# Means of squares by full-width products with ones, and the root by logarithm, exponential and a Newton step

## The chip, the cores and the metric

One core of one Trainium2 chip runs the whole kernel. The metric is the device time of one execution in microseconds. The kernel before takes 2461.68 us, the median of three runs (2461.52 to 2463.72). Single-precision data throughout; the large products are made as three products of high and low parts of the operands, so that their sum has single precision.

## The reference

One layer of a hybrid decoder, for a prompt of 1024 tokens and 8 single-token samples that share the weights: a combined input projection, three branches (a gated short convolution, a Mamba-2 state-space scan with 32 heads in 4 groups, and cross-attention to 256 memory tokens), gates, a merging projection, and a SwiGLU feed-forward network. The change touches two norms of it:

```python
def rmsnorm(x, w, eps=RMS_EPS):
    y = xf * lax.rsqrt(jnp.mean(xf * xf, axis=-1, keepdims=True) + eps)
    return (y * w)

y_ssd = (y_ssd + ssm_d[:, None] * xs) * jax.nn.silu(z)
y_b = group_rmsnorm(y_ssd, ssm_norm_w, SSM_GROUPS) @ w_ssm_out   # 4 groups of 512 channels
...
xp = xp + h
xp = xp + swiglu(rmsnorm(xp, norm_ffn_w[l]), w_ffn_gate[l], w_ffn_up[l], w_ffn_down[l])
```

## The kernel before

**Layout.** Channels lie on the 128 partitions, tokens along the free axis: 1024 of the prompt and 8 of the samples, 1032 columns (`TT`), in three pieces of 344 (`CW`) for the large products of TensorE (`gemm`, L205) or, in the feed-forward part, two halves of 516 (`HT`), each of 2 x 258 (`HC`). A norm over channels is therefore a sum over partitions.

**Order.** The program is emitted as a list of background pieces (`pend`) that are woven between the products of `gemm`: at certain k-steps of a product the next piece is emitted (`tick`). A `None` in the list lets one such place pass. A scheduler then sets each engine's order by its own plan of times. Each engine runs its queue strictly in order; an instruction that waits holds up all behind it. DMAs that the code issues on `SY` go through SyncE's queue (SP), also in order.

**The state-space stage.** For each head group `g` (512 channels, four tiles `xg[0..3]` of 128x1032) `load_group` (L1376 to L1380) loads the x tiles from `xs_d`, `ssd_pieces` runs eight chunks of 128 tokens (each begins with four transposes of x, `xp`, L989), and at the group's end `z_pieces` adds the skip term (L1112, on DVE), multiplies by the gate (L1115, DVE), squares on ACT (L1120, L1122) and sums the four squares into one tile `sqa` (L1123, DVE). `group_norm` follows:

- `sums` (L1136 to L1144): nine products with a block of 128 columns of `sqa` as the stationary operand and a single column of ones as the moving one (`psny`), which leave the sums with tokens on partitions, 128x9; then on these few values the mean, Sqrt on ACT (with a load of its table), reciprocal and a Newton step on DVE.
- `spread` (L1152 to L1156): nine transposes of the roots, each broadcast along the free axis, which turn them back to tokens along the free axis on all partitions (`psnr`); ACT copies them into `sqa`.
- `scale` (L1160, L1163): four DVE operations x = x * weight * root, and a store of each tile to `yb_d` on SP. The x tiles of the next group use the buffers of these tiles, and their loads (L1380) stand behind the stores on SP.

The other engines' work in this time: TensorE runs the products of the projections `wq` (`ps_q`) in group 0 and of the output projections `wo` (`po`) in groups 1 to 3, DVE the low parts of their weights (L155) and activations (L165), ACT the high parts, exponentials of the scan (L969), and evictions. After the last group come the transposes of the q rows of the samples (`psqr`, copied by ACT into `qrows`) and of the keys (`pskT`, evicted by ACT into `kTh`), the loads of the first keys and values (`kv_ahead`) and cross-attention. Small PSUM tiles (`sm_ps`: psny, psnr, xp, psqr, pskT and others) have two buffers.

**The feed-forward norm.** The merging products (L1823) write the sum x tile by tile; `norm_half` (L1766 to L1786) does the same as above for one half of the columns: six products (`psf`, L1772), the root on 128x6 values, six transposes (`psr`, L1785), two ACT copies into `rf`. Half 0 is woven into the merging products of half 1; half 1 comes just ahead of the first products of the feed-forward network (`g0e`, `u0e`, L253). `normed` (L1790) then scales x, and its forms (high and low parts, sums of blocks for Strassen products) feed those products.

**Engines.** The names in the profile: PE is TensorE, DVE is VectorE, ACT is ScalarE, POOL is GpSimd, SP is SyncE. In the state-space stage GpSimd has small scalings of 128x512 (L1000, L1049).

Of the kernel before, what the change touches and what calls it, by code (L numbers as in the profile page):

```python
# [12 lines left out]
ALU = mybir.AluOpType  # L13
# [30 lines left out]
def tile_kernel(ctx: ExitStack, tc, a, o):  # L44
# [53 lines left out]
    def rsqrt(pool, out, src, n, shape, name):  # L98
# [7 lines left out]
        V.scalar_tensor_tensor(out, t, 1.5, out, op0=ALU.add, op1=ALU.mult)  # L106

# [317 lines left out]
    with tc.tile_pool(name="p0", bufs=1) as p0:  # L425
# [27 lines left out]
        for key, src, n in (  # L453
            ("mem", a["norm_mem_w"], 8),
            ("ffn", a["norm_ffn_w"], 8),
            ("scw", a["sc_conv_w"], 24),
            ("scb", a["ssm_conv_b"], 24),
            ("ssn", a["ssm_norm_w"], 16),
# [650 lines left out]
    def z_pieces(g, xg, hold):  # L1109
        def piece(t):  # L1110
            zs = hold.pop(t)
            V.scalar_tensor_tensor(  # L1112
# [6 lines left out]
            if t == 0:  # L1119
                S.activation(sqa[:, :TT], xg[t], AF.Square)  # L1120
            else:
                S.activation(zs, xg[t], AF.Square)  # L1122
                V.tensor_add(sqa[:, :TT], sqa[:, :TT], zs)  # L1123
# [5 lines left out]
    def group_norm(g, xg, hold):  # L1129

        starts = [i * P for i in range(NCK)] + [TT - P]

        def sums():
            ps = sm_ps(f"psny{g}")
            for i, c in enumerate(starts):
                PE.matmul(ps[:, i : i + 1], hold["q"][:, c : c + P], ones[:, 0:1], start=True, stop=True)  # L1136
            t = hold["r"] = ev_tile(f"nr{g}")
            r, v, s_ = t[:, :9], t[:, 9:18], t[:, 18:27]
            V.tensor_scalar(v, ps[:, :9], 1.0 / 512, EPS, op0=ALU.mult, op1=ALU.add)
            S.activation(s_, v, AF.Sqrt)  # L1140
            V.reciprocal(r, s_)
            V.tensor_mul(s_, r, r)
            V.scalar_tensor_tensor(s_, v, -0.5, s_, op0=ALU.mult, op1=ALU.mult)
            V.scalar_tensor_tensor(r, s_, 1.5, r, op0=ALU.add, op1=ALU.mult)  # L1144

        def spread():
            n = hold["n"] = hold["q"]
            for half in range(2):
                ps = sm_ps(f"psnr{g}{half}")
                for i in range(4):  # L1150
                    j = half * 4 + i
                    PE.transpose(ps[:, i * P : (i + 1) * P], bc(hold["r"][:, j : j + 1], [P, P]), ident)  # L1152
                S.copy(n[:, half * 512 : (half + 1) * 512], ps)
            ps = sm_ps(f"psnr{g}2")
            PE.transpose(ps[:, :P], bc(hold["r"][:, 8:9], [P, P]), ident)
            S.copy(n[:, T:TT], ps[:, P - NS : P])  # L1156

        def scale():
            for t in range(4):
                V.scalar_tensor_tensor(  # L1160
                    xg[t], xg[t], par("ssn", g * 4 + t), hold["n"][:, :TT], op0=ALU.mult, op1=ALU.mult
                )
                SY.dma_start(yb_d[g * 4 + t], xg[t])  # L1163

        return [sums, None, spread, scale]
# [312 lines left out]
    for g in range(GROUPS):  # L1478
# [8 lines left out]
        if g == GROUPS - 1:  # L1487
            norm[1] = lambda: kv_ahead(0)
# [277 lines left out]
    def norm_half(half, sq):  # L1766
        rfs[half] = ev_tile(f"rf{half}")
        t = rfs[half]
        starts = [n * HC + c for n in range(2) for c in (0, P, HC - P)]
        ps = sm_ps(f"psf{half}")  # L1770
        for i, c in enumerate(starts):
            PE.matmul(ps[:, i : i + 1], sq[:, c : c + P], ones[:, 0:1], start=True, stop=True)  # L1772
        r, v = t[:, 600:606], t[:, 606:612]
        s_ = t[:, 612:618]
        V.tensor_scalar(v, ps[:, :6], 1.0 / D, EPS, op0=ALU.mult, op1=ALU.add)
        S.activation(s_, v, AF.Sqrt)
        V.reciprocal(r, s_)
        V.tensor_mul(s_, r, r)
        V.scalar_tensor_tensor(s_, v, -0.5, s_, op0=ALU.mult, op1=ALU.mult)
        V.scalar_tensor_tensor(r, s_, 1.5, r, op0=ALU.add, op1=ALU.mult)  # L1780
# [423 lines left out]
```

## Time and profile before

| | |
|---|---|
| median of three runs | 2461.68 us |
| profiled execution, its own time | 2464.7 us |
| its span | 2463.0 us |
| granted TensorE clock, mean | 0.999 of full |
| ScalarE busy | 1084.4 us (44%) |
| group norms: last add of group 0, 1, 2, 3 starts at | 1076.61, 1167.24, 1250.33, 1339.80 us |
| feed-forward norm, first product of half 0 and 1 | 1715.21 and 1762.17 us |
| TensorE's largest wait in the state-space stage and attention | 2.6 us, for the first attention products (`psa`) |

Times are from one profiled execution, counted from the start of its span. A row of the timeline gives the start, the duration, the engine, the source line, the operation, what it writes and reads, and how many of its kind were merged into the row; brackets give the idle time of the engine just before it and what ended that. One single-precision product is two MATMUL instructions in such a row.

### The profile page before, as it was taken

How to read it: one execution, taken by the hardware profiler on the slowest of the kernel's cores; microseconds unless marked ns; L12 is line 12 of the kernel's file. 1: busy time of each engine (PE TensorE's matmuls, PEld its weight loads, DVE VectorE, ACT ScalarE, POOL GpSimd, SP SyncE). 2: the span in 40 equal slices, each digit the busy share in tenths (PEclk: the TensorE clock that was granted, in tenths of full speed). 3: DMA queues.
4: the chain of work that ended last, by engine and by line, in shares of the span. 5: the costliest groups of instructions: out<-in, count | busy, mean ns of one | idle time of the engine just before them, and what ended most of it. 6: DMA issues, size and time to landing. Idle time of an engine off the chain costs nothing.

```text
span 2463.0 us, 45791 instructions
## 1 busy us (share of the span) xinstructions
PE 2426.6 (99%) x19020; PEld 2363.1 (96%) x19020; DVE 1599.3 (65%) x2589; ACT 1084.4 (44%) x1747; POOL 107.4 (4%) x163
## 2 busy tenths in 40 slices
PE   8999999999999999999999999999999999999998
PEld 6999999999999999888998988999999999999998
DVE  6744677777777675568677763554777555567855
ACT  6634555455453543656555442213443333343423
POOL 0000000000000000212211000000000000000000
PEclk9999999999999999999999999999999999999999
DMA  6355323444343345767886897855444323254621
GB/s 206 129 164 161 121 86 110 133 138 129 115 152 116 108 123 178 219 219 256 266 279 214 267 316 239 275 192 162 145 153 131 102 92 106 89 184 145 189 88 76
DMA packets 359606, 404.81 MB, mean 164 GB/s; under 512 B 16110, under 2 KB 286046, under 8 KB 359391
## 3 DMA queue, kind: packets, MB, share of 16 engines
q1 hardware_dynamic: 334374, 339.69, 44.2%
q10 hardware_dynamic: 25025, 62.21, 6.7%
q8 instruction: 149, 2.44, 0.4%
q14 instruction: 58, 0.48, 0.1%
HBM read 286.74 MB, written 115.32 MB: 163 GB/s over the span
## 4 chain that ended last, share of the span: by engine, by line
PE 85%; DMA 6%; DVE 5%; ACT 3%; issue 1%; SPq 0%; DVEq 0%; ACTq 0%; POOL 0%
PE po L205 11%; PE pm L1823 4%; PE ps_q L205 3%; PE pss L1036 1%; PE py L1023 1%; DMA qb<-qs_d 1%; PE ps_z L205 1%; PE po L1015 1%; DMA in<-yb_d 1%; PE G16m L253 1%; PE Z14m L253 1%; PE Z2m L253 1%; PE d00m L253 1%; PE d16m L253 1%; PE d14m L253 1%
## 5 line engine op out<-in xcount | busy, mean ns | idle before, releaser
L968 ACT ACTIVATE r<-r,acum 128x128 f32<-128x128 f32 x256 | 79.1, 392 | 4.2 <-DMA r<-ac_d 3.5
L758 DVE SCALAR_TENSOR_TENSOR ax<-u,prm,ax 128x1024 f32<-128x1024 f32 x44 | 56.4, 1281 | 0.4 <-ACT ax L755 0.3
L909 ACT ACTIVATE st<-st,es 128x128 f32<-128x128 f32 x128 | 41.3, 392 | 26.1 <-DMA st<-in_state_ssm_dram 21.5
L1000 POOL TENSOR_TENSOR xdd<-xdt,decst 128x512 f32<-128x512 f32 x32 | 37.1, 1159 | 290.6 <-DVE xdt L996 290.6
L994 DVE TENSOR_TENSOR r<-r,cbm 128x1024 f32<-128x1024 f32 x32 | 39.1, 1223 | 2.2
L911 DVE SCALAR_TENSOR_TENSOR st<-sr,dts,st 128x128 f32<-128x128 f32 x128 | 40.2, 347 | 0.4
L1019 DVE TENSOR_TENSOR y<-po,ea 128x512 f32<-128x512 f32 x28 | 19.3, 688 | 28.4 <-PE po L1015 27.1
L915 DVE SCALAR_TENSOR_TENSOR sr<-st,sr 128x128 f32<-128x128 f32 x128 | 35.4, 287 | 1.1
L1456 DVE TENSOR_TENSOR yr<-po,yr 128x1032 f32<-128x1032 f32 x8 | 9.8, 1230 | 40.3 <-PE po L205 22.6
L1023 PE MATMUL py<-r,xdt 128*64 128x128 f32 x512 | 35.0, 279 | 0.0
L1036 PE MATMUL pss<-xdd,bT 128*128 128x512 f32 x64 | 34.2, 616 | 0.7 <-ACT bT L993 0.4
L1830 DVE TENSOR_TENSOR x<-pm,xT 128x516 f32<-128x516 f32 x16 | 11.1, 695 | 36.2 <-PE pm L1823 36.2
L969 ACT ACTIVATE r<-r 128x1024 f32<-128x1024 f32 x32 | 33.9, 1058 | 0.7
L1049 POOL TENSOR_TENSOR s<-s,cdec 128x512 f32<-128x512 f32 x28 | 33.1, 1182 | 2.4 <-DVE s L1042 2.2
L993 ACT COPY bT<-bp 128x128 f32<-128x128 f32 x32 | 8.5, 264 | 54.3 <-DVE cbm L991 54.2
L1023 PEld LDWEIGHTS py<-r,xdt 128*64 128x64 f32 x512 | 27.3, 136 | 4.2 <-issue 0.9
L1752 DVE TENSOR_TENSOR gt<-po,gt 128x1032 f32<-128x1032 f32 x8 | 9.9, 1233 | 32.1 <-PE po L205 30.6
L1557 DVE SCALAR_TENSOR_TENSOR kc<-kc,qb 128x256 f32<-128x256 f32 x64 | 23.7, 421 | 9.7 <-DMA qb<-qs_d 8.3
L1015 PE MATMUL po<-bc,s 128*128 128x128 f32 x224 | 29.8, 276 | 0.0
L1015 PEld LDWEIGHTS po<-bc,s 128*128 128x128 f32 x224 | 28.3, 191 | 0.6 <-DVE s L1042 0.5
L755 ACT ACTIVATE ax<-u,prm 128x1024 f32<-128x1024 f32 x22 | 27.4, 1246 | 2.3 <-DVE u L368 1.1
L761 DVE SCALAR_TENSOR_TENSOR ax<-u,prm,ax 128x1032 f32<-128x1032 f32 x22 | 28.3, 1289 | 0.0
(9217 smaller groups left out, 9097.9 us busy)
## 6 DMA issues: line engine op xcount, KB each, us to landing
r<-ac_d SPq DMA_DIRECT2D x32, 512.0 KB
gt_d<-G ACTq DMA_DIRECT2D x24, 516.0 KB
gt<-gt_d SPq DMA_DIRECT2D x24, 516.0 KB
xs_d<-ax ACTq DMA_DIRECT2D x22, 516.0 KB
x<-xs_d SPq DMA_DIRECT2D x16, 516.0 KB
zs<-zs_d SPq DMA_DIRECT2D x16, 516.0 KB
yb_d<-x SPq DMA_DIRECT2D x16, 516.0 KB
in<-yb_d SPq DMA_DIRECT2D x16, 516.0 KB
```

Of the source, the lines that this page charges most:

```text
L205: PE.matmul(ps[:, n, :CW], wt[:, ks], x[:, n * CW : (n + 1) * CW], start=(k == 0 and i == 0), stop=(k == nk - 1 and i == 2),)
L253: PE.matmul(ps[:, n, :HC], wt[:, ks], x[:, n * HC : (n + 1) * HC], start=(start and kt == 0 and i == 0), stop=(kt == 3 and i == 2), skip_g ...
L758: V.scalar_tensor_tensor(acc[:, :T], u[:, j : j + T], w[j], acc[:, :T], op0=ALU.mult, op1=ALU.add)
L909: S.activation(st[:, i], st[:, i], AF.Copy, scale=es[:, g * 4 + i, b : b + 1])
L911: V.scalar_tensor_tensor(st[:, i], rb, dts[:, g * 4 + i, b : b + 1], st[:, i], op0=ALU.mult, op1=ALU.add)
L968: S.activation(r[:, j, :], r[:, j, :], AF.Relu, scale=-1.0, bias=acum[:, c, h : h + 1])
L994: V.tensor_tensor(r, r, bc(cbm.unsqueeze(1), [P, HPG, P]), op=ALU.mult)
L1000: G.tensor_tensor(b3(xdd, HPG), b3(xdt, HPG), bc(decst[:, c, hs].unsqueeze(2), [P, HPG, 64]), op=ALU.mult)
L1015: PE.matmul(po[:, t * P : (t + 1) * P], state["s"][:, t * P : (t + 1) * P], bcg[1][:, cs], start=True, stop=True,)
L1023: PE.matmul(py[hp : hp + 64, (h // 2) * P : (h // 2 + 1) * P], xdt[:, h * 64 : (h + 1) * 64], r[:, (h % 2) * 4 + h // 2, :], start=True, s ...
L1036: PE.matmul(pss, bT, xdd, start=True, stop=True)
L1823: PE.matmul(ps[:, n, :HC], wt[:, ks], x[:, half * HT + n * HC : half * HT + (n + 1) * HC], start=(k == 0 and i == 0), stop=(k == KD - 1 an ...
```

## The change

Both norms now get their means by products with a 128x128 matrix of ones, filled with the reciprocal of the number of channels, as the stationary operand and the squares as the moving one. The result has the mean of a token on every partition, so nothing has to be turned back. The root is taken on all of it, 128x1032 or 128x516: ACT makes the logarithm, the exponential of minus half of it, and its square; DVE makes a Newton step in the form (v r r - 3) r, which is -2 times the reciprocal root. The norm's weights are multiplied by -0.5 once to make up for that; the weights' rows are put side by side so that one instruction does it.

In `group_norm` three products of 344 columns take the place of nine products and nine transposes; DVE adds epsilon on the way out of PSUM, into a tile that the group no longer needs (of `y`, or in the last group of `zs`). The second and third of the four squares are added on GpSimd instead of DVE. The matrix of ones is filled anew at group 0 (1/512) and after group 3 (1/1024). The list's slots become two pieces of means, one empty, and the scaling; the last group's `kv_ahead` stands one slot later. In `norm_half` two products of 258 columns take the place of six products and six transposes, and ACT reads them from PSUM, adding epsilon as its bias.

The order that the scheduler makes of it is shown at three places. Line numbers in rows of the change are those of the changed kernel, which are 7 to 9 higher than before for the same line. The first is TensorE at the end of group 0; psny are the means, L205 and L213 the products of the projection. Before:

```order
L205 MATMUL ps_q_12233<-xnl_128,wq4h 128x344 x3
L205 MATMUL ps_q_12233<-xnh_127,wq4l 128x344 x3
L205 MATMUL ps_q_12233<-xnh_129,wq4h 128x344 x3
L205 MATMUL ps_q_12233<-xnl_130,wq4h 128x344 x3
L205 MATMUL ps_q_12233<-xnh_129,wq4l 128x344 x3
L1136 MATMUL psny_12256<-ones,sqa_12182 128x1 x9
L205 MATMUL ps_q_12233<-xnh_131,wq4h 128x344 x3
L205 MATMUL ps_q_12233<-xnl_132,wq4h 128x344 x3
L205 MATMUL ps_q_12233<-xnh_131,wq4l 128x344 x3
```

After:

```order
L213 MATMUL ps_q_12233<-xnl_128,wq4h 128x344
L1144 MATMUL psny_12259<-sqa_12182,ones 128x344
L1144 MATMUL psny_12262<-sqa_12182,ones 128x344
L213 MATMUL ps_q_12233<-xnl_128,wq4h 128x344
L1144 MATMUL psny_12274<-sqa_12182,ones 128x344
L213 MATMUL ps_q_12233<-xnl_128,wq4h 128x344
L213 MATMUL ps_q_12233<-xnh_127,wq4l 128x344 x3
L213 MATMUL ps_q_12233<-xnh_129,wq4h 128x344 x3
L213 MATMUL ps_q_12233<-xnl_130,wq4h 128x344 x3
```

The means now stand 14 products of 344 columns earlier in TensorE's queue (463 products of L205, counted from one place ahead of it in both, where 477 stood), and the nine transposes behind them are gone. Ahead of the third transpose of the next group's first chunk stand 572 such products where 567 stood; in the next two groups it is 941 for 927 and 1260 for 1251.

The second is DVE at the same place, from the first group's skip terms to the scaling; x_11368, x_11370, x_11372 and x_11374 are the four x tiles. Before:

```order
L1112 SCALAR_TENSOR_TENSOR x_11372<-x_11372,dpar,y_11570 128x1032
L1123 TENSOR_TENSOR sqa_12182<-sqa_12182,zs_12114 128x1032
L1115 TENSOR_TENSOR x_11372<-x_11372,zs_12184 128x1032
L1112 SCALAR_TENSOR_TENSOR x_11374<-x_11374,dpar,y_11570 128x1032
L155 TENSOR_TENSOR wq6l<-wq6r,wq6h 128x1024
L1123 TENSOR_TENSOR sqa_12182<-sqa_12182,zs_12184 128x1032
L1115 TENSOR_TENSOR x_11374<-x_11374,zs_12199 128x1032
L1066 COPY y_12432<-ys 128x4x8
L1123 TENSOR_TENSOR sqa_12182<-sqa_12182,zs_12199 128x1032
L1139 TENSOR_SCALAR nr_12266<-psny_12256 128x9
```

After:

```order
L1121 SCALAR_TENSOR_TENSOR x_11372<-x_11372,dpar,y_11570 128x1032
L1121 SCALAR_TENSOR_TENSOR x_11374<-x_11374,dpar,y_11570 128x1032
L1124 TENSOR_TENSOR x_11372<-x_11372,zs_12184 128x1032
L1124 TENSOR_TENSOR x_11374<-x_11374,zs_12199 128x1032
L163 TENSOR_TENSOR wq6l<-wq6r,wq6h 128x1024
L1132 TENSOR_TENSOR sqa_12182<-sqa_12182,zs_12199 128x1032
L1145 TENSOR_SCALAR y_11570<-psny_12259 128x344
L1145 TENSOR_SCALAR y_11570<-psny_12262 128x344
L1145 TENSOR_SCALAR y_11570<-psny_12274 128x344
L113 TENSOR_TENSOR sqa_12182<-y_11570,sqa_12182 128x1032
L114 SCALAR_TENSOR_TENSOR sqa_12182<-sqa_12182,y_11570 128x1032
```

Two of three adds have left DVE; they stand on GpSimd directly after the scaling of the state of the last chunk. The five tiny operations on nr (one of them in the rows above) are replaced by three evictions of 344 columns and two operations of 1032. The third is ACT in group 3, where the q rows and the keys of cross-attention follow. Before:

```order
L1122 ACTIVATE zs_14878<-x_14114 128x1032
L1140 ACT_TABLE_LOAD
L1140 ACTIVATE nr_14934<-nr_14934 128x9
L1453 COPY yr_15004<-po_14867 128x1032
L1454 DMA yr_d<-yr_15004 128x1032
L1153 COPY sqa_14870<-psnr_14963 128x512
L1153 COPY sqa_14870<-psnr_14969 128x512
L1156 COPY sqa_14870<-psnr_14975 128x8
L1530 CAST vh<-vv_14950 128x1024
L1173 COPY qrows<-psqr_15008 8x512
L1173 COPY qrows<-psqr_15014 8x512
L154 CAST wo15h<-wo15r 128x1024
```

After:

```order
L1537 CAST vh<-vv_14906 128x1024
L162 CAST wo14h<-wo14r 128x1024
L1180 COPY qrows<-psqr_14940 8x512
L110 ACT_TABLE_LOAD
L110 ACTIVATE sqa_14819<-zs_14821 128x1032
L1180 COPY qrows<-psqr_14946 8x512
L111 ACT_TABLE_LOAD
L111 ACTIVATE zs_14827<-sqa_14819 128x1032
L1545 CAST kTh<-pskT_14976 128x4x128
L112 ACTIVATE sqa_14819<-zs_14827 128x1032
L1545 CAST kTh<-pskT_14983 128x4x128
L1537 CAST vh<-vv_14990 128x1024
```

The table load of Sqrt gives way to one for the logarithm and one for the exponential, and the evictions of the q rows and of the first key tiles now stand between and behind these and the three full-width operations. In groups 0 to 2 the same five instructions stand in the same order, and the reload for the exponentials of the next chunk, which stood there before (L969), is gone.

```diff
@@ -104,6 +104,14 @@
         V.tensor_mul(t, out, out)
         V.scalar_tensor_tensor(t, v, -0.5, t, op0=ALU.mult, op1=ALU.mult)
         V.scalar_tensor_tensor(out, t, 1.5, out, op0=ALU.add, op1=ALU.mult)
+
+    def minus_two_roots(v, r, t):
+
+        S.activation(t, v, AF.Ln)
+        S.activation(r, t, AF.Exp, scale=-0.5)
+        S.activation(t, r, AF.Square)
+        V.tensor_mul(t, v, t)
+        V.scalar_tensor_tensor(t, t, -3.0, r, op0=ALU.add, op1=ALU.mult)
 
 
 
@@ -453,9 +461,9 @@
         for key, src, n in (
             ("mem", a["norm_mem_w"], 8),
             ("ffn", a["norm_ffn_w"], 8),
+            ("ssn", a["ssm_norm_w"], 16),
             ("scw", a["sc_conv_w"], 24),
             ("scb", a["ssm_conv_b"], 24),
-            ("ssn", a["ssm_norm_w"], 16),
             ("xcw", a["ssm_conv_w"], 96),
         ):
             flat_src = src
@@ -1109,6 +1117,7 @@
     def z_pieces(g, xg, hold):
         def piece(t):
             zs = hold.pop(t)
+            hold["zs"] = hold.get("zs", [])[-1:] + [zs]
             V.scalar_tensor_tensor(
                 xg[t], xg[t], dpar[:, g * 4 + t : g * 4 + t + 1], hold["y"][:, t, :], op0=ALU.mult, op1=ALU.add
             )
@@ -1120,7 +1129,7 @@
                 S.activation(sqa[:, :TT], xg[t], AF.Square)
             else:
                 S.activation(zs, xg[t], AF.Square)
-                V.tensor_add(sqa[:, :TT], sqa[:, :TT], zs)
+                (G if t < 3 else V).tensor_tensor(sqa[:, :TT], sqa[:, :TT], zs, op=ALU.add)
             if t + 2 < 4:
                 z_load(g, t + 2, hold)
 
@@ -1128,41 +1137,39 @@
 
     def group_norm(g, xg, hold):
 
-        starts = [i * P for i in range(NCK)] + [TT - P]
-
-        def sums():
-            ps = sm_ps(f"psny{g}")
-            for i, c in enumerate(starts):
-                PE.matmul(ps[:, i : i + 1], hold["q"][:, c : c + P], ones[:, 0:1], start=True, stop=True)
-            t = hold["r"] = ev_tile(f"nr{g}")
-            r, v, s_ = t[:, :9], t[:, 9:18], t[:, 18:27]
-            V.tensor_scalar(v, ps[:, :9], 1.0 / 512, EPS, op0=ALU.mult, op1=ALU.add)
-            S.activation(s_, v, AF.Sqrt)
-            V.reciprocal(r, s_)
-            V.tensor_mul(s_, r, r)
-            V.scalar_tensor_tensor(s_, v, -0.5, s_, op0=ALU.mult, op1=ALU.mult)
-            V.scalar_tensor_tensor(r, s_, 1.5, r, op0=ALU.add, op1=ALU.mult)
-
-        def spread():
-            n = hold["n"] = hold["q"]
-            for half in range(2):
-                ps = sm_ps(f"psnr{g}{half}")
-                for i in range(4):
-                    j = half * 4 + i
-                    PE.transpose(ps[:, i * P : (i + 1) * P], bc(hold["r"][:, j : j + 1], [P, P]), ident)
-                S.copy(n[:, half * 512 : (half + 1) * 512], ps)
-            ps = sm_ps(f"psnr{g}2")
-            PE.transpose(ps[:, :P], bc(hold["r"][:, 8:9], [P, P]), ident)
-            S.copy(n[:, T:TT], ps[:, P - NS : P])
-
-        def scale():
-            for t in range(4):
+
+        def means(i):
+            c = slice(i * CW, (i + 1) * CW)
+            ps = sm_ps(f"psny{g}{i}")
+            PE.matmul(ps[:, :CW], ones, hold["q"][:, c], start=True, stop=True)
+            V.tensor_scalar(hold["v"][0][:, c], ps[:, :CW], EPS, None, op0=ALU.add)
+
+        def first():
+            if g == 0:
+
+                V.memset(ones, 1.0 / 512)
+                V.memset(root, EPS)
+                both = prm[:, PC["ffn"] : PC["ssn"] + 16]
+                V.tensor_scalar(both, both, -0.5, None, op0=ALU.mult)
+
+            hold["v"] = hold["zs"] if g == GROUPS - 1 else [hold["y"][:, i, :] for i in range(2)]
+            means(0)
+            means(1)
+
+        def second():
+            means(2)
+            if g == GROUPS - 1:
+                V.memset(ones, 1.0 / D)
+            minus_two_roots(*hold.pop("v"), hold["q"][:, :TT])
+
+        def scale(ts):
+            for t in ts:
                 V.scalar_tensor_tensor(
-                    xg[t], xg[t], par("ssn", g * 4 + t), hold["n"][:, :TT], op0=ALU.mult, op1=ALU.mult
+                    xg[t], xg[t], par("ssn", g * 4 + t), hold["q"][:, :TT], op0=ALU.mult, op1=ALU.mult
                 )
                 SY.dma_start(yb_d[g * 4 + t], xg[t])
 
-        return [sums, None, spread, scale]
+        return [first, second, None, lambda: scale(range(4))]
 
     def q_rows():
         t = ev_tile("qrows", (NS, D))
@@ -1485,7 +1492,7 @@
         pend.extend(pieces[-3:])
         norm = group_norm(g, xg, hold)
         if g == GROUPS - 1:
-            norm[1] = lambda: kv_ahead(0)
+            norm[2] = lambda f=norm[2]: (f and f(), kv_ahead(0))
         pend.extend(z_pieces(g, xg, hold) + [None] + norm)
     pace[:] = len(pend) / (len(fillers) + KD + 2) + 1e-6, 0.0
     while fillers or pend:
@@ -1764,26 +1771,19 @@
     rfs = [None, None]
 
     def norm_half(half, sq):
-        rfs[half] = ev_tile(f"rf{half}")
-        t = rfs[half]
-        starts = [n * HC + c for n in range(2) for c in (0, P, HC - P)]
-        ps = sm_ps(f"psf{half}")
-        for i, c in enumerate(starts):
-            PE.matmul(ps[:, i : i + 1], sq[:, c : c + P], ones[:, 0:1], start=True, stop=True)
-        r, v = t[:, 600:606], t[:, 606:612]
-        s_ = t[:, 612:618]
-        V.tensor_scalar(v, ps[:, :6], 1.0 / D, EPS, op0=ALU.mult, op1=ALU.add)
-        S.activation(s_, v, AF.Sqrt)
-        V.reciprocal(r, s_)
-        V.tensor_mul(s_, r, r)
-        V.scalar_tensor_tensor(s_, v, -0.5, s_, op0=ALU.mult, op1=ALU.mult)
-        V.scalar_tensor_tensor(r, s_, 1.5, r, op0=ALU.add, op1=ALU.mult)
-        for n in range(2):
-            ps = sm_ps(f"psr{half}{n}")
-            for i in range(3):
-                c = starts[i]
-                PE.transpose(ps[:, c : c + P], bc(r[:, 3 * n + i : 3 * n + i + 1], [P, P]), ident)
-            S.copy(t[:, n * HC : (n + 1) * HC], ps[:, :HC])
+        rfs[half] = out = ev_tile(f"rf{half}")
+        t, r = sq[:, :HT], sq[:, HT:TT]
+        pss = [sm_ps(f"psf{half}{n}")[:, :HC] for n in range(2)]
+        cs = [slice(n * HC, (n + 1) * HC) for n in range(2)]
+        for ps, c in zip(pss, cs):
+            PE.matmul(ps, ones, sq[:, c], start=True, stop=True)
+        for ps, c in zip(pss, cs):
+            S.activation(t[:, c], ps, AF.Ln, bias=root)
+        S.activation(r, t, AF.Exp, scale=-0.5)
+        S.activation(t, r, AF.Square)
+        for ps, c in zip(pss, cs):
+            V.scalar_tensor_tensor(t[:, c], ps, EPS, t[:, c], op0=ALU.add, op1=ALU.mult)
+        V.scalar_tensor_tensor(out[:, :HT], t, -3.0, r, op0=ALU.add, op1=ALU.mult)
 
     def normed(m, half):
         t = x2[m][:, HS[half]]
```

## The prediction

> **What bounds the kernel now.** The page comes first: TensorE is busy for 2426.6 of 2463.0 us, and the chain that ended last is mostly its work. So only two things count: products taken off TensorE, and places where TensorE is made to wait.
>
> ```profile
> PE 2426.6 (99%) x19020; PEld 2363.1 (96%) x19020; DVE 1599.3 (65%) x2589; ACT 1084.4 (44%) x1747; POOL 107.4 (4%) x163
> ```
>
> The view of waits of TensorE is second. Neither the sums of squares (psny, psf) nor the spread roots (psnr, psr) is in it; but one row of the state-space stage is: the third transpose of a head group's first chunk waits for its x tile.
>
> ```profile
> PE xp L989 <- DMA x<-xs_d: 1.6, 1, 1.6
> ```
>
> The timeline around the end of group 0 shows what that tile waits for. Columns: start, duration, engine, line, operation, result<-inputs.
>
> ```profile
> 1067.15 1.29 DVE L1112 SCALAR_TENSOR_TENSOR x<-x,dpar,y 128x1032 f32<-128x1032 f32 x1
> 1067.38 1.05 ACT L1122 ACTIVATE zs<-x 128x1032 f32<-128x1032 f32 x1
> ...
> 1076.61 1.23 DVE L1123 TENSOR_TENSOR sqa<-sqa,zs 128x1032 f32<-128x1032 f32 x1 [1.04 <-ACT zs L1122]
> ...
> 1078.04 2.06 PE L1136 MATMUL psny<-ones,sqa 128*128 128x1 f32 x18
> ...
> 1080.37 1.28 ACT L1140 ACT_TABLE_LOAD   x1 [3.80 <-DVE nr L1139]
> 1080.52 0.64 PE L205 MATMUL ps_q<-xnl,wq4h 128*128 128x344 f32 x3
> 1080.99 0.63 PE L205 MATMUL ps_q<-xnh,wq4l 128*128 128x344 f32 x3
> ...
> 1081.67 0.21 ACT L1140 ACTIVATE nr<-nr 128x9 f32<-128x9 f32 x1
> ...
> 1082.88 1.06 PE L1152 MATMUL psnr<-ident,nr 128*128 128x128 f32 x8
> ...
> 1084.50 0.63 PE L205 MATMUL ps_q<-xnl,wq4h 128*128 128x344 f32 x3
> ...
> 1084.74 4.91 DVE L1160 SCALAR_TENSOR_TENSOR x<-x,prm,sqa 128x1032 f32<-128x1032 f32 x4 [2.00 <-ACT sqa L1156]
> ...
> 1086.06 4.01 SPq L1163 DMA_DIRECT2D yb_d<-x  x4
> ...
> 1090.16 2.57 SPq L1380 DMA_DIRECT2D x<-xs_d  x2
> ...
> 1097.74 0.33 PE L989 MATMUL xp<-ident,x 128*128 128x128 f32 x1 [1.65 <-DMA x<-xs_d]
> ```
>
> Read downwards it is one chain: the last add ends at 1077.84, the root and its spread take 6.9 us, the scaling follows at 1084.74, its stores go out on SP, the next group's x tiles queue behind them, and TensorE arrives 1.65 us too soon. Only in group 0 does the chain come late; but there no time saved by TensorE ahead of 1097.74 can show.
>
> **The work that TensorE loses.** Psny costs 1080.52 - 1078.04 less three other products (three take 0.47, from 1080.52 to 1080.99): 2.0 us. Psnr costs 1084.50 - 1082.88 less 0.47: 1.15. The new products are plain f32, like those of the chunk states:
>
> ```profile
> 1133.84 1.02 PE L1036 MATMUL pss<-xdd,bT 128*128 128x512 f32 x2
> ...
> 1134.30 0.72 PE L205 MATMUL ps_q<-xnl,wq7h 128*128 128x344 f32 x1
> ...
> 1134.86 0.63 PE L205 MATMUL ps_q<-xnh,wq7l 128*128 128x344 f32 x3
> ```
>
> One product of 512 columns (two instructions) and one L205 (0.16) fill 1.02, so 512 columns cost 0.86, 344 cost 0.58, and three 1.74. A group saves 3.15 - 1.74 = 1.4, four save 5.6.
>
> The FFN norm's halves likewise:
>
> ```profile
> 1715.21 1.39 PE L1772 MATMUL psf<-ones,sq 128*128 128x1 f32 x12
> ...
> 1716.79 0.40 PE L1823 MATMUL pm<-mgs6l,wm10h 128*128 128x258 f32 x2
> ...
> 1719.64 0.87 PE L1785 MATMUL psr<-ident,rf 128*128 128x128 f32 x6
> ```
>
> Psf takes 1.58 less one pair of products (0.24), 1.34; psr about 0.8. Two products of 258 columns cost 0.87. A half saves 1.3, both 2.6. **All savings together: 8.2 us**, if TensorE waits nowhere that it did not.
>
> **The root's own chain, group 0.** Before, from the last add to the scaling: 6.9 us. After, by rows above: the first two products 1.2; the eviction of the second frees a PSUM buffer for the third (an eviction of 344 columns I put at 0.5, the nearest row being L1139's 0.17 and a 128x512 one's 0.69), so the third mean is ready some 2.5 after the add. Then Ln, 1.06 like the square L1122; the load of the exponential's table, 1.28; Exp 1.06; Square 1.06; a multiply 1.2 and a STT 1.3 on DVE. With gaps of 0.1 to 0.2: 9.6 us, **2.7 more**. The rows of before that give way are tiny ones; ten times as many elements go through ACT and DVE. A second load per group does not add to ACT's work, for the exponential's reload in the next chunk goes; it moves onto this chain.
>
> [...]
>
> **The adds on GpSimd.** Two of three go there. No row shows such an add; 128x512 ones stand here:
>
> ```profile
> 1134.95 1.05 POOL L1000 TENSOR_TENSOR xdd<-xdt,decst 128x512 f32<-128x512 f32 x1 [3.13 <-DVE xdt L996]
> ...
> 1141.20 1.22 DVE L994 TENSOR_TENSOR r<-r,cbm 128x1024 f32<-128x1024 f32 x1
> ...
> 1141.36 1.96 POOL L1000 TENSOR_TENSOR xdd<-xdt,decst 128x512 f32<-128x512 f32 x1 [4.37 <-DVE xdt L996]
> ...
> 1142.33 2.08 DVE L165 TENSOR_TENSOR b02l<-in,b02h 128x1032 fp32r<-128x1032 f32 x1
> ```
>
> 1.05 for 512 gives 2.1 for 1032, against 1.23 on DVE. And the two engines exclude each other: the GpSimd operation that started during L994 lasted 0.91 longer, until 1143.32, and DVE's next operation ended 1.09 after that, taking 2.08 where others take 1.22. All of DVE's work in this stretch (L1112, L1115, L155) reads two SBUF operands. So I let an add wait for DVE's current operation and hold up the next. From 1068.43 (the square's end): add 1 from 1069.6 to 1071.7, the multiplies of x2 and x3 then, add 2 from 1074.1 to 1076.2, the split of wq6 to 1077.3, the last add to 1078.5: 0.7 later than before. With no exclusion it would end at about 1076.5, 1.3 earlier; those are the ends.
>
> [...]
>
> So the scaling of group 0 comes 0.7 + 2.7 = 3.4 later (1.4 to 4), and with it loads and transpose. The order has five more L205 products ahead of that transpose (572 for 567): 0.8 us of TensorE work done meanwhile. **Group 0: +2.6**, between +0.6 and +3.2; its 1.4 saved is swallowed by the wait.
>
> **Groups 1 and 2.** Last add, scaling, third transpose:
>
> ```profile
> 1167.24 1.22 DVE L1123 TENSOR_TENSOR sqa<-sqa,zs 128x1032 f32<-128x1032 f32 x1
> 1175.93 3.70 DVE L1160 SCALAR_TENSOR_TENSOR x<-x,prm,sqa 128x1032 f32<-128x1032 f32 x3 [3.94 <-ACT sqa L1156]
> 1188.14 0.27 PE L989 MATMUL xp<-ident,x 128*128 128x128 f32 x1
> 1250.33 1.22 DVE L1123 TENSOR_TENSOR sqa<-sqa,zs 128x1032 f32<-128x1032 f32 x1
> 1260.70 3.70 DVE L1160 SCALAR_TENSOR_TENSOR x<-x,prm,sqa 128x1032 f32<-128x1032 f32 x3 [2.00 <-ACT sqa L1156]
> 1272.94 0.27 PE L989 MATMUL xp<-ident,x 128*128 128x128 f32 x1
> ```
>
> No wait there, but little slack: from scaling to transpose 12.2 in both, against 13.0 in group 0, where it waited; I take 0.4. Group 1's root takes 7.5 now, 9.6 after, and the adds 0.7 to 1.9: 2.8 to 4 later. The order puts 14 more products (2.2 us) ahead of the transpose. 3.6 - 0.4 - 2.2 = **+1.0** (-1.4 to +2.0). Group 2's root takes 9.1 now, because ACT was busy: 1.2 to 3.2 later, 0.4 slack, 9 more products (1.4): **+0.3** (-1.4 to +1.4).
>
> **Group 3** has no next group. But ACT's queue there also evicts transposes, and PSUM's small tiles have two buffers:
>
> ```profile
> 1339.80 1.23 DVE L1123 TENSOR_TENSOR sqa<-sqa,zs 128x1032 f32<-128x1032 f32 x1
> ...
> 1341.48 2.06 PE L1136 MATMUL psny<-ones,sqa 128*128 128x1 f32 x18
> ```
>
> In the changed order TensorE's means of group 3 are followed at once by the transposes of the q rows and of the first keys, with two runs of five L205 products (0.8 us each) between them, and on ACT both table loads stand between the evictions that free their buffers. The second tile of the q rows waits behind Ln (1.06 + its load), the first of the keys behind Exp (1.06 + 1.28), the second behind Square (1.06): about 1.3 + 1.2 + 0.5 = 3.0; the first mean adds 0.4, the saving takes 1.4: **+2.0** (-1.4, if the products move past, to +4, with the adds' 1.9).
>
> **FFN norm.** Half 1:
>
> ```profile
> 1762.17 1.43 PE L1772 MATMUL psf<-ones,sq 128*128 128x1 f32 x12
> ...
> 1766.23 1.42 DVE L1790 SCALAR_TENSOR_TENSOR x<-x,prm,rf 128x516 f32<-128x516 f32 x2 [1.37 <-ACT rf L1786]
> ```
>
> After: products 0.9, two Ln 0.7, load 1.3, Exp and Square 0.6 each (as 128x516 casts), two evicting STTs and one more 1.6: 5.7 where 4.1 stood. What is late is the forms of half 1, on a DVE nearly full after it:
>
> ```profile
> 1780.00:1800.00 20.00, 20.00 (x168) 20.00 (x168) 19.49 (x31) 14.01 (x24) 0.00 (x0) 1.00 0.57 192
> ```
>
> TensorE waits for none of them now; I give back 0.5. Half 0 has products of the second half to hide it. **-2.6 + 0.5 = -2.1** (-2.6 to 0).
>
> **Sum:** 2.6 + 1.0 + 0.3 + 2.0 - 2.1 = **+3.8** on the profiled execution's 2464.7, so 2468.5; that execution is 3.0 above the median of 2461.68, so the runs should show **2465.5**. The terms' ends added up give -5 to +11.
>
> **Rivals.** (1) *The saving shows in full.* For it: the norms never stood among TensorE's waits. Against: the chain of group 0 was late already, and it grows. With waits of at most half the saving: -8.2 to -4, about 2455. (2) *Slower clearly.* One mechanism: the exclusion in groups 1 to 3, where DVE also has the gate products and the splits of wo. If each add there waits for one DVE operation and holds up another, two cost 2 x (2.1 + 1.2) = 6.6 in the chain where 2.5 stood, 4.1 more, of which I booked 0.7 to 1.9. It decides once the scaling of groups 1 and 2 comes over 4.5 later: then the sum gains some 2 a group, +10, 2471.5. For it: the pair of rows at 1141. Against: group 0's walk, where an add mostly fills time in which the last square is awaited. (3) *The adds run freely*: 1.3 less in each group against 0.7 more, so 2 less per group where TensorE waits: about -2, 2459.5.
>
> **Chances.** Forecast 0.45, full saving 0.25, clear loss 0.20, free adds 0.10. About 0.2% (4.9 us) is what a measurement of this kernel can tell from no change. The forecast, +1 to +7, I split 0.25 within and 0.20 slower; the full saving 0.22 faster, 0.03 within; clear loss all slower; free adds all within. That is 0.22 faster, 0.38 same, 0.40 slower. Range 2455.5 to 2473, from the middle of the full saving to just above the clear loss; the forecast's own is 2462.5 to 2468.5.
>
> **What would show it.** In the changed profile: a wait of TensorE of about 2.8 at group 0's first mean; a larger wait than 1.65 at the third transpose of group 1's first chunk, and new ones in the next two; GpSimd adds over 2.1 us long with DVE operations of 2 us beside them; key transposes that wait on ACT. If the waits at the transposes stay under 2 and none stand at the means, the chain was not what counts, and the time lies near 2455.

## The result, and the profile after

The changed kernel is slower: 2480.43 us in the median of four runs against 2462.7 for the kernel before, a ratio of 1.0066 with a 95% interval of 1.0045 to 1.0086; a second set of six runs gave 1.0067 (1.0052 to 1.0081). That is 16 us. The profiled execution took 2475.6 us, its span is 2473.9, 10.9 more than before. The forecast was 2465.5 with a range of 2455.5 to 2473: the time lies outside.

The page of the changed kernel shows that TensorE's work did shrink, and that GpSimd has 31 us more:

```profile
span 2473.9 us, 45563 instructions
...
PE 2424.8 (98%) x18908; PEld 2356.1 (95%) x18908; DVE 1609.4 (65%) x2581; ACT 1099.6 (44%) x1748; POOL 138.1 (6%) x171
```

The view of TensorE's waits has a new first row. Columns: what waited, for whom, total us, times, longest.

```profile
PE psny L1144 <- DVE sqa L1132: 10.9, 4, 3.1
...
PE pss L1044 <- ACT bT L1001: 2.8, 3, 1.3
PE xp L997 <- DMA x<-xs_d: 2.6, 2, 1.6
...
PE pskT L1543 <- DVE kTl L1546: 1.1, 2, 0.9
PE pskT L1543 <- ACT qrows L1180: 1.1, 1, 1.1
```

At each of the four group norms TensorE stands 2.1 to 3.1 us at the first mean, waiting for the last add of squares. Before, no row of that kind was there. The timeline at the end of group 0 says why the add is late:

```profile
1068.96 2.49 DVE L1121 SCALAR_TENSOR_TENSOR x<-x,dpar,y 128x1032 f32<-128x1032 f32 x2
...
1070.33 9.27 POOL L1132 TENSOR_TENSOR sqa<-sqa,zs 128x1032 f32<-128x1032 f32 x2 [8.85 <-ACT zs L1131]
1071.37 2.37 DVE L1124 TENSOR_TENSOR x<-x,zs 128x1032 f32<-128x1032 f32 x2
...
1073.65 1.22 DVE L163 TENSOR_TENSOR wq6l<-wq6r,wq6h 128x1024 fp32r<-128x1024 f32 x1
...
1079.63 1.23 DVE L1132 TENSOR_TENSOR sqa<-sqa,zs 128x1032 f32<-128x1032 f32 x1 [4.76 <-POOL sqa L1132]
...
1080.91 1.43 PE L1144 MATMUL psny<-sqa,ones 128*128 128x344 f32 x4 [3.12 <-DVE sqa L1132]
...
1084.89 1.28 ACT L111 ACT_TABLE_LOAD   x1
...
1090.91 4.91 DVE L1167 SCALAR_TENSOR_TENSOR x<-x,prm,sqa 128x1032 f32<-128x1032 f32 x4
```

The view of that line on GpSimd, for the two adds of group 0 (count, shortest/median/longest in ns), splits the 9.27:

```profile
L1132 POOL TENSOR_TENSOR sqa<-sqa,zs x2: 2362/4596/6829, 1070.3 to 1077.2; 128x1032 f32<-128x1032 f32 x2
```

The first add began at 1070.33 and took 6.83 us. VectorE ran five operations one after another from 1068.96 on, each at its usual length, and ended the last at 1074.87; the add ended 2.3 us after that, the length of an undisturbed one (2.36). So the add seems to have got nothing done while VectorE's operations followed on each other. VectorE then stood idle for 4.76 us. In group 2 the adds did get in between, and VectorE paid as well: two of its operations, 1.2 us alone, took 2.31 and 3.42 beside them. No run shows why the adds got in there and not in group 0.

```profile
1256.08 6.80 POOL L1132 TENSOR_TENSOR sqa<-sqa,zs 128x1032 f32<-128x1032 f32 x2 [9.79 <-ACT zs L1131]
...
1258.31 2.31 DVE L1124 TENSOR_TENSOR x<-x,zs 128x1032 f32<-128x1032 f32 x1
1260.54 3.42 DVE L163 TENSOR_TENSOR wo07l<-wo07r,wo07h 128x1024 fp32r<-128x1024 f32 x1
```

One of these waits cost more than its length. The view by stretches around group 1's first mean (columns: stretch, length, busy time of PE, PEld, DVE, ACT, POOL, then the granted clock):

```profile
1168.00:1172.00 4.00, 4.00 (x27) 4.00 (x27) 2.56 (x3) 3.11 (x3) 3.92 (x2) 1.00 0.02 8
1172.00:1176.00 4.00, 1.09 (x5) 0.78 (x4) 1.82 (x2) 0.00 (x0) 2.14 (x1) 0.84 0.61 158
1176.00:1182.00 6.00, 6.00 (x19) 4.56 (x18) 2.10 (x5) 1.06 (x1) 0.00 (x0) 0.54 0.99 324
1182.00:1186.00 4.00, 2.96 (x20) 2.67 (x19) 1.52 (x2) 3.65 (x5) 0.00 (x0) 1.00 1.06 288
```

TensorE is idle for 2.9 us, and is then granted about half its clock until it is back at 1182: 3.4 us of its work are lost on top of the wait (the clock's shortfall, 4 x 0.16 + 6 x 0.46). Such a dip of the clock stands once more at 300, without a wait, in a place that the change leaves alone, and costs 1.7. The kernel before has no such dip before its last microseconds. In ten executions of the changed kernel, those of its repetition below included, the time goes roughly with the mean clock: 2475.6 at 0.998, 2478.2 to 2482.4 at 0.996 or 0.997, 2481.7 at 0.995, 2486.0 at 0.994. A thousandth of 2,480 us is 2.5.

### The profile page after: what moved, and what is told of

It reads as the page before. It is cut to its first block, busy times and chain, and to the rows that moved or that the text cites. A ratio compares the mean times of both kernels' runs of the same rounds, so it can differ in the third digit from the quotient of the medians.

```text
span 2473.9 us, 45563 instructions
## 1 busy us (share of the span) xinstructions
PE 2424.8 (98%) x18908; PEld 2356.1 (95%) x18908; DVE 1609.4 (65%) x2581; ACT 1099.6 (44%) x1748; POOL 138.1 (6%) x171
## 4 chain that ended last, share of the span: by engine, by line
PE 79%; DVE 8%; DMA 7%; ACT 4%; issue 2%; POOL 1%; SPq 0%; POOLq 0%; DVEq 0%; ACTq 0%
PE po L213 9%; PE pm L1823 4%; PE ps_q L213 2%; PE py L1031 1%; PE ps_z L213 1%; PE pss L1044 1%; PE X17m L261 1%; PE G16m L261 1%; PE Z14m L261 1%; PE Z2m L261 1%; PE d00m L261 1%; PE C0m L261 1%; PE Z6m L261 1%; PE Z10m L261 1%; PE C5m L261 1%
## 5 line engine op out<-in xcount | busy, mean ns | idle before, releaser
L1132 POOL TENSOR_TENSOR sqa<-sqa,zs 128x1032 f32<-128x1032 f32 x8 | 29.8, 3728 | 36.3 <-ACT zs L1131 36.0
```

## The experiments

The theory from this profile (A): the adds on GpSimd are what costs, by TensorE's waits at the means. Rivals: the root's longer chain (B), a lower clock for some other reason (C).

**All adds back on VectorE.** The rest of the change stays.

```diff
-                (G if t < 3 else V).tensor_tensor(sqa[:, :TT], sqa[:, :TT], zs, op=ALU.add)
+                V.tensor_add(sqa[:, :TT], sqa[:, :TT], zs)
```

> The changed kernel with all three adds of squares back on VectorE; the rest of the change stays. Theory A (the GpSimd adds starve beside VectorE's own operations and TensorE stands 10.9 us at the four first means): the waits at the means fall from 10.9 to under 3 us, the four last adds come 3 to 5 us earlier, and the time falls 8 to 11 us below that of the changed kernel, to a ratio of 1.000 to 1.003 against the kernel before. Rival B (the longer chain of the root, with its second table load, is what costs): the waits move from the means to the x tiles of the next group, and the time falls less than 4 us. Rival C (TensorE's granted clock is lower in the changed kernel, 0.995 to 0.998 against 0.999): the clock stays at 0.996 and the time within 4 us of the changed kernel's.

Ratio 0.9984 (0.9975 to 0.9993): faster than the kernel before, and some 20 us faster than the changed one. The waits at the means are gone altogether, and the clock is 0.998 to 1.000 in all twelve runs. A named the cause but allowed it half its size. B's waits are there, without deciding; they stand at the x tiles:

```profile
PE xp L997 <- DMA x<-xs_d: 4.7, 3, 2.0
```

Against 1.6 before, that fits the longer root: in group 0 the scaling starts 11.2 us after the last add instead of 6.9.

**The adds on GpSimd alone**, in the kernel before: the same line, the other way round.

> The kernel before with one edit, the second and third squares added on GpSimd. Theory A: 6 to 11 us slower than before (ratio 1.0025 to 1.0045), with GpSimd adds of 2.4 to 7 us and waits of TensorE at the sums of squares or at the x tiles. Rival B: within 2 us of before. Rival C: no statement on the time, but a granted clock like that of before, 0.999.

Ratio 1.009 (1.0077 to 1.0103), 22 us: more than the whole change loses. Waits and clock of the profiled execution, the stretches around group 0's sums:

```profile
PE psny L1136 <- DVE sqa L1123: 12.8, 4, 3.4
```

```profile
1074.00:1078.00 4.00, 0.85 (x6) 0.56 (x5) 1.39 (x2) 0.00 (x0) 2.61 (x3) 1.00 0.80 249
1078.00:1086.00 8.00, 8.00 (x37) 7.98 (x38) 0.89 (x5) 1.49 (x2) 0.00 (x0) 0.57 0.45 162
```

All four groups show such a dip; with the clock's shortfall summed over stretches of 2 us they cost 3.4, 5.1, 3.4 and 3.4 us, 15.3 together, where this span exceeds that of before by 19.1. The waits of 12.8 do not come on top in full: TensorE is busy for 13.3 us longer than before and idle for only 5.8 more (2439.9 of 2482.1 us against 2426.6 of 2463.0), so part of them stands in the place of idle time that was elsewhere. The mean clock is 0.992 to 0.994 in the five runs. That A fell short by twofold and C had no reason for the clock led to a new pair: TensorE's own idle time lowers its clock (E), or GpSimd's work does (F).

**Either half of the change alone.** First the feed-forward norm, with the group norms as before and these lines behind the last group's spread:

```diff
+            if g == GROUPS - 1:
+                V.memset(ones, 1.0 / D)
+                V.memset(root, EPS)
+                fw = prm[:, PC["ffn"] : PC["ffn"] + 8]
+                V.tensor_scalar(fw, fw, -0.5, None, op0=ALU.mult)
```

Then the group norms with adds on VectorE, and the feed-forward norm as before:

```diff
-                V.memset(ones, 1.0 / D)
+                V.memset(ones, 1.0)
...
-                both = prm[:, PC["ffn"] : PC["ssn"] + 16]
+                both = prm[:, PC["ssn"] : PC["ssn"] + 16]
```

> The kernel before with the new feed-forward norm alone, the group norms as before. By the prediction's term 2.1 us faster (0 to 2.6), a ratio of 0.9990 to 1.0000, with a few tenths of waits ahead of the first products of the feed-forward network. Theory A and rival B say the same; rival C: if the full-width products lower the clock it is slower.

> The changed group norms with adds on VectorE, and the feed-forward norm as before. Theory A: 2 us slower than e1_dve_adds, for the saving of the halves is missing. Rival B: 4 us or more slower than the kernel before, by waits at the x tiles and in group 3's transposes.

The first gives 0.9990 (0.9981 to 0.9998), 2.5 us, as the term said; the second 0.9991 (0.9982 to 0.9999), 2.2 us, where B wanted it slower than the kernel before. Together they make up the gain of both at once, 4 us, within the intervals.

**One add on GpSimd instead of two.**

```diff
-                (G if t < 3 else V).tensor_tensor(sqa[:, :TT], sqa[:, :TT], zs, op=ALU.add)
+                (G if t == 1 else V).tensor_tensor(sqa[:, :TT], sqa[:, :TT], zs, op=ALU.add)
```

> The changed kernel with only the second square's add on GpSimd, the third and fourth on VectorE. Theory A (a GpSimd add that starts while VectorE runs operation after operation lasts until they pause): this one add lasts 3 to 7 us, the last add ends 1 to 4 us later than in e1_dve_adds, TensorE waits 2 to 8 us at the four means together, and the time lies 4 to 12 us above e1_dve_adds. Rival D (each add costs its own length, so half the adds cost half): the add lasts 2.4 to 3.3 us, and the time lies half way between the changed kernel and e1_dve_adds.

Ratio 1.0029 (1.002 to 1.0039), 11 us above the version without. By the time alone A and D both hold, for half way would be 1.0025. The durations of the four adds decide; none is as short as D needs (3.3 us), the nearest by 0.1:

```profile
L1132 POOL TENSOR_TENSOR sqa<-sqa,zs x4: 3392/3447/6832, 1067.4 to 1344.5; 128x1032 f32<-128x1032 f32 x4
```

**Filling the wait** with products of no use, in the kernel with the adds on GpSimd and in the changed one (12 and `ps[:, 3 * P :]` there).

```diff
             ps = sm_ps(f"psny{g}")
+            with tc.issue_after(hold["sq"]):
+                for _ in range(14):
+                    PE.matmul(ps[:, P : 2 * P], ones, tri, start=True, stop=True)
```

> e2_pool_adds with 14 products of no use (3 us of TensorE's time) ahead of each group's sums of squares, where TensorE stood idle for about 3 us and was granted half its clock for some 7 us afterwards. Theory E (the idle time itself lowers the clock): the waits are filled at no cost, the dips of the clock behind them vanish, the mean clock returns from 0.994 to 0.998 or more, and the time falls 8 to 14 us below e2_pool_adds. Rival F (GpSimd's work lowers the clock, not TensorE's idle time): the clock stays at 0.994 and the time rises by up to 12 us. Outside group 1, where the order puts them 18 products ahead of the sums, the waits at the sums should be under 1 us.

> The changed kernel with 12 products of no use (2.6 us) ahead of each group's first mean. Theory E: the mean clock rises from 0.995 to 0.998 in its runs to 0.998 or more in nearly all, and the time falls 3 to 8 us below that of the changed kernel. Rival F: no change of clock, the time equal or up to 5 us above.

Both missed: 1.0137 (1.0123 to 1.015) and 1.0126 (1.0112 to 1.014), some 12 and 15 us slower than without. The scheduler put the idle products where real ones had stood, and those behind the sums, so that the wait stayed (11.7 and 14.0 us in total):

```profile
1072.52 3.29 PE L1137 MATMUL psny<-tri,ones 128*128 128x128 f32 x28
...
1077.85 2.35 PE L1139 MATMUL psny<-ones,sqa 128*128 128x1 f32 x18 [2.04 <-DVE sqa L1123]
```

So these two do not tell E from F. They do show that the scheduler fills time by its own plan. The changed kernel's order shows that too: as if the adds on GpSimd ended early, it sets the means 14, 15, 22 and 22 products of 344 columns earlier in TensorE's order than the version with the adds on VectorE does (463, 820, 1138 and 1486 against 477, 835, 1160 and 1508 ahead of them). At 0.16 us each, TensorE comes 2.2 to 3.5 us sooner to data that come later.

**A root without the second table load**: Sqrt on ScalarE, a reciprocal on VectorE in the group norms, adds on VectorE.

```diff
-        S.activation(t, v, AF.Ln)
-        S.activation(r, t, AF.Exp, scale=-0.5)
+        S.activation(t, v, AF.Sqrt)
+        V.reciprocal(r, t)
```

> e1_dve_adds with Sqrt on ScalarE and a reciprocal on VectorE in the place of the logarithm and exponential in the group norms, so that no table load stands in the root's chain. Rival B (the second table load and the long chain are what is left of the loss): the waits at the x tiles (4.7 us in e1_dve_adds) fall under 2.5 and the time falls 2 to 4 us. Theory A: within 2 us of e1_dve_adds. If the reciprocal of 128x1032 takes more than 2.4 us the chain is longer than with the second load and the time rises.

Ratio 1.0033 (1.0021 to 1.0046), 12 us above the logarithm and exponential. The reciprocal's price decides, the case named last:

```profile
L111 DVE RECIPROCAL y<-sqa x3: 6591/6593/6603, 1081.5 to 1273.4; 128x1032 f32<-128x1032 f32 x3
```

Three of the four are in this row; the fourth, in group 3, takes 6.60. B is therefore not tested by this run: its chain is longer, not shorter.

**Idle time without GpSimd**, in the kernel before.

```diff
+            if t == 3:
+                one = sqa[:, 0:1]
+                for f in (AF.Ln, AF.Exp, AF.Sqrt, AF.Square):
+                    S.activation(one, one, f)
```

> The kernel before, nothing on GpSimd, with four ScalarE operations on one column of the summed squares ahead of each group's sums (logarithm, exponential, root, square, which give the column back). They need three table loads of 1.28 us, which the scheduler's order leaves out of account, so that TensorE should stand idle for 3 to 4 us at each group's sums. Theory E (TensorE's idle time itself lowers its clock): the clock falls to 0.993 to 0.996 with dips right behind the sums, and the time rises by the waits, 10 to 16 us, and by 5 to 14 us more. Rival F (GpSimd's work, not idle time, lowers the clock): the clock stays at 0.998 to 0.999 and the time rises by the waits alone.

Ratio 1.0035 (1.0021 to 1.0049), and the runs lie far apart: 2466.73 at a clock of 0.999, 2472.56 and 2474.03 at 0.997, 2473.09 at 0.996, 2482.99 at 0.993. The waits were much shorter than expected, since the scheduler does count the four operations and set the sums 14 products later in group 0:

```profile
PE psny L1140 <- ACT sqa L1127: 3.3, 4, 1.0
```

Yet in the profiled execution (that of 0.993) the clock dips behind all four sums, as these stretches after group 0's show:

```profile
1082.00:1084.00 2.00, 0.98 (x9) 0.85 (x8) 0.00 (x0) 1.06 (x3) 0.00 (x0) 1.00 0.39 153
1084.00:1086.00 2.00, 2.00 (x16) 2.00 (x17) 0.32 (x2) 0.21 (x1) 0.00 (x0) 0.93 0.00 0
1086.00:1088.00 2.00, 2.00 (x9) 1.94 (x9) 0.57 (x4) 0.00 (x0) 0.00 (x0) 0.50 0.00 0
1088.00:1090.00 2.00, 2.00 (x13) 1.76 (x12) 0.00 (x0) 1.24 (x4) 0.00 (x0) 0.72 0.00 0
```

No GpSimd work stands there, so F falls. Two more dips, 1.7 each, follow waits of 1.98 and 2.19 us in the attention that came after, where GpSimd is idle too. At the sums only 1 us of wait stands, though; behind it follow the nine one-column products, 2 us. The question left was whether these count as idle time.

**The same wait ahead of dense products**: the same four operations in the version with full-width means and adds on VectorE.

> e1_dve_adds (full-width means, all adds on VectorE) with the same four operations on one column and three table loads ahead of each group's means as in e9_blind. Theory E, with the nine one-column products of the kernel before counting as near-idle time: the waits are about 1 us at each group's first mean as there, but dense products follow, so the clock stays at 0.998 or more and the time lies 3 to 7 us above e1_dve_adds. If instead a wait of 1 us is enough by itself: a clock of 0.993 to 0.997 as in e9_blind and 8 to 20 us above e1_dve_adds.

The clock is 0.998 to 1.000 in all eleven runs and there is no dip ahead of the last microseconds, although the waits are longer than in the experiment before, one of them 2.6 us:

```profile
PE psny L1148 <- ACT sqa L1136: 5.0, 4, 2.6
```

The ratio is 1.0006 (0.9998 to 1.0015), about 5 us above the version without the four operations. So four operations and three loads on ScalarE do not lower the clock by themselves, and the case named last, a wait of 1 us being enough, does not hold.

By itself this does not show that a wait with dense products behind it is safe. In the profiles of two other experiments a wait of that kind was followed by a dip that cost 1.7 us: 1.95 us at an x tile with all adds on VectorE (clock 0.50 at 1102 to 1104), and 1.97 us at group 2's first mean with one add on GpSimd (0.52 at 1262 to 1264). What speaks for the one-column products is the run with the new feed-forward norm alone, whose group norms are those of the kernel before, with nothing of theirs on GpSimd. Behind group 1's sums, without any wait, its clock dips, and 1.7 us of work are lost:

```profile
1166.43 2.12 PE L1136 MATMUL psny<-ones,sqa 128*128 128x1 f32 x18
```

```profile
1166.00:1168.00 2.00, 2.00 (x19) 1.93 (x18) 1.46 (x2) 0.00 (x0) 0.00 (x0) 1.00 0.74 225
1168.00:1170.00 2.00, 2.00 (x11) 2.00 (x12) 0.98 (x6) 0.21 (x1) 0.00 (x0) 0.68 0.94 361
1170.00:1172.00 2.00, 2.00 (x8) 2.00 (x8) 0.00 (x0) 0.00 (x0) 0.00 (x0) 0.50 1.01 410
```

So E holds as far as it goes: dips follow TensorE's idle time, be it a wait for GpSimd's adds (2.91 us), for an x tile (1.95) or in the attention (1.98), and one followed 2.12 us of one-column products without a wait. That the clock counts such products as idle is my guess; no run shows it. Not every such stretch brings a dip, and which does is not shown.

**The changed kernel again**, unedited.

> The changed kernel unedited, for pairs of time and granted clock beside those that stand. Theory E: its executions spread by several us, each 0.001 of mean clock being worth about 2.5 us (0.001 of 2,480), and at a clock of 0.999 the time would be about 2473.

Six runs from 2478.22 to 2485.99 at 0.994 to 0.997, ratio 1.0067. None reached 0.999, so the time there is only worked out. The profiled execution, 2479.22 at 0.997, has dips of 1.7 behind the first three means and the one at 300: 6.8 us, where the one before it had 5.1. Its span is 3.5 longer, so the dips account for half of that.

## Why the prediction was wrong

- **The sum without the clock** came near, in part by luck. The dips cost 5.1 us of the profiled execution's 10.9 (3.4 in group 1 and 1.7 at 300); the other 5.8 stand against the forecast's 3.8. But the parts are off. One and the same merging product, before and after, starts 13.5 us later:

```profile
1665.01 0.40 PE L1823 MATMUL pm<-mgs1h,wm00h 128*128 128x258 f32 x2
```

```profile
1678.49 0.40 PE L1823 MATMUL pm<-mgs1h,wm00h 128*128 128x258 f32 x2
```

At 1032, ahead of group 0's end, such a product was 1.5 late (the dip at 300). So the four groups and the attention lost 11.9, or 8.5 without group 1's dip, where 5.9 was forecast. The feed-forward norm then gained 1.0 by 1825 where 2.1 was forecast, and 1.5 more came back in the rest, which the change leaves alone.
- **The step that failed** is the one that turns waits into time. "Group 0: +2.6" and its like price an idle TensorE at the length of the wait. The wait at group 0's first mean was forecast as about 2.8 and measured as 3.12. What no term has is that a wait of about 3 us can be followed by a dip of the clock (0.68, 0.50, 0.50 and 0.61 in the four stretches of 2 us from 1174 to 1182) that costs another 3.4, at up to four places and not in every execution: the 5 us between the profiled execution and the median go with the clock, 0.998 in the one and 0.995 or 0.996 in the other three. The range's upper end had no term for that. The sum also had the waits at the wrong place. It put the delay of groups 0 to 2 at the transposes of x, more than 1.65 us in the first and new waits in the next two; there the trace has 1.56, 1.04 and none. At the first means it expected about 2.8 in group 0 and 0.4 in group 3, and nothing in groups 1 and 2; there it has 3.12, 2.91, 2.74 and 2.10.
- **The adds on GpSimd** were the right place, and the adds and VectorE's operations do lengthen each other (adds of 2.36 to 6.83 us; 2.31 and 3.42 for operations of 1.2), but not by the rule of the forecast. "An add waits for VectorE's current operation and holds up the next" gave 2.1 to 3.3 us an add; the first in group 0 waited for all operations of a run and took 6.83. The row at 1141 was read as if it told who goes first; it only showed that one of the two takes longer, 1.96 us where 1.05 is usual. What had been the rival of a clear loss named this exclusion, and 4.1 us more of chain. The loss came by the means, not by the x tiles that it and the forecast looked at in groups 1 and 2.
- **What was put on the order**: the means 14 products (2.2 us) early in group 0 gave the wait forecast there. For groups 1 and 2 only the products ahead of the transposes were counted, 14 and 9 more, as work done meanwhile. That the means come sooner there too, by 7 and 5 products in the two traces, has no term.
- **The root's chain**: 9.6 us in group 0 by rows, 10.05 measured (1080.86 to 1090.91). The load of the exponential's table stands in it with 1.28, and the next operation follows 0.01 after it ended.
- **Group 3**: waits of 1.3, 1.2 and 0.5 at the transposes were forecast; they are 1.06 and 0.89, and 0.2 at the last. The rows, the second a wait for a buffer that VectorE and ScalarE empty together:

```profile
1362.82 0.66 PE L1543 MATMUL pskT<-ident,kk 128*128 128x128 f32 x4 [1.06 <-ACT qrows L1180]
...
1366.39 0.66 PE L1543 MATMUL pskT<-ident,kk 128*128 128x128 f32 x4 [0.89 <-DVE kTl L1546]
```

- **The feed-forward norm**: forecast -2.6 + 0.5; alone it gave 2.5 (0.5 to 4.7 by the interval). The chain of half 1 was put at 5.7 us and took 5.75, as the first two rows show. The half microsecond given back was too little: of the 2.55 that both halves gained, 1.5 were lost again by 1825. The last two rows have two new waits, 1.1 us together; the timeline of before marks none there. The second stands behind a table load of 1.28 us on ScalarE. That late forms cause them is not shown.

```profile
1774.36 1.06 PE L1779 MATMUL psf<-sq,ones 128*128 128x258 f32 x4
...
1780.11 1.42 DVE L1790 SCALAR_TENSOR_TENSOR x<-x,prm,rf 128x516 f32<-128x516 f32 x2
...
1817.32 0.51 PE L261 MATMUL g0m<-T30h,g0Th 128*128 128x258 f32 x2 [0.28 <-DVE g0e L367]
...
1821.32 0.48 PE L261 MATMUL g0m<-T40h,g0Dh 128*128 128x258 f32 x2 [0.83 <-ACT g0e L1924]
```

- **The rivals**: the full saving did not come, but "the adds run freely", 2 us faster, is near what the version with adds on VectorE does by avoiding them: 4 us faster.

What stays open is why the clock dips in one execution of a kernel and not in the next. The dip at 300 came in some profiled executions with adds on GpSimd and in some without, among them the kernel before with the four operations put in. No run tests what starts it, but tiny products stand just ahead of it, four runs of 0.66 us, 8 columns wide, within 5 us; the rows are from the run of the new group norms alone:

```profile
298.66 0.66 PE L742 MATMUL ps_ex<-ident,exs 8*128 8x8 f32 x8
...
299.92 0.66 PE L742 MATMUL ps_ex<-ident,exs 8*128 8x8 f32 x8
```

```profile
300.00:302.00 2.00, 2.00 (x16) 1.97 (x17) 1.32 (x6) 0.14 (x1) 0.17 (x3) 0.71 0.00 0
302.00:304.00 2.00, 2.00 (x12) 2.00 (x11) 1.53 (x5) 1.66 (x3) 0.00 (x0) 0.50 0.36 147
```

The kernel before has the same products there and no dip.

## What to carry to other kernels

Where TensorE is busy 99% of the time, price a new wait of 2 to 3 us at up to about twice its length, an estimate from group 1 here (2.91 us of wait, 3.4 of clock behind it): the clock is part of the cost, and the spread between executions with their mean clocks is where one sees it. Before moving an elementwise operation to GpSimd, look at what VectorE does in the same microseconds, not at its share of time: beside a run of VectorE's operations an add took up to 6.83 us, in a gap 2.36. A scheduler that plans with a free engine may also bring its consumers forward. A full-width product instead of tiny products and transposes was worth 4 us here, once the adds were left where they were.

## What the runs showed of the hardware

- Half the clock after idle time: the dips within the profiled executions, those in the last microseconds aside, cost 1.7, 3.4 or 5.1 us (1.68 to 1.72, 3.40 to 3.42 and 5.10 to 5.12 by stretches of 2 us), multiples of 1.7. Whole stretches inside them show a clock of 0.50, at which these are 3.4, 6.8 or 10.2 us of half the clock. In one execution a wait of 2.9 us was followed by a dip and waits of 3.1 and 2.7 were not; in others a dip followed 1 us with 2 us of one-column products behind it, 2.12 us of such products alone, and waits of 1.95 to 2.2 us, while one of 2.6 had none. How long TensorE has to stand idle for a dip, and whether thin products count as idle, no run shows.
- A GpSimd add of 128x1032 takes 2.36 us undisturbed and up to 6.83 beside a run of VectorE operations that read two operands from SBUF. In the kernel before, between 1000 and 1330, the scalings of 128x512 on GpSimd (L1000, L1049) took 1.95 to 2.03 us in the eight cases where they began during a VectorE operation of that kind (L155, L165, L994), and 1.04 or 1.05 in all others, beside VectorE operations that read PSUM (L1042, L1019) too.
- A reciprocal of 128x1032 on VectorE takes 6.6 us, more than five times a multiply (1.23).
